# Moving sigmoid products and norm powers to GpSimd in a decoder layer of stick-breaking attention

## The chip, the core and the metric

The kernel runs on one core of a Trainium2 chip. The metric is the device time of one execution in microseconds (us); lower is better. The core has a matrix engine (PE in the rows; PEld is its weight load), a vector engine (DVE), a scalar engine (ACT), GpSimd (POOL), and a queue engine that issues the DMAs (SP). PE writes its results to PSUM, which DVE and ACT can read; everything else lies in SBUF.

## The reference

One decoder layer on an input of 2048 tokens by 1024 features, all in float32. Cut to what matters here:

```python
proj = x @ w_in                    # q, k, v (8 heads x 64), conv gates and h, pooling input
# stick-breaking attention, causal, per head, for query t and keys s < t
z = (q @ k.T) * 64 ** -0.5
log_om = where(s < t, log_sigmoid(-z), 0)
tail = reverse_cumsum(log_om) - log_om
a = where(s < t, exp(log_sigmoid(z) + tail), 0)
o = a @ v
# beside it: a short gated convolution and a multi-window pooling
mix = concat(o, conv, pooled)      # 1024 wide
mix = mix * rsqrt(mean64(mix * mix) + 1e-6) * gain      # norm of each group of 64
x = layer_norm(alpha * x + mix @ w_o)
x = layer_norm(alpha * x + relu(x @ w_up) ** 2 @ w_down)
```

A weight of the attention is thus a sigmoid of z times a product, over the keys between s and t, of sigmoids of -z.

## The kernel before

**Precision.** Each float32 operand of a large matmul is split in a rounded half (an ACT copy) and a remainder (a subtraction on DVE or GpSimd), and three matmuls stand for one. `load` (L163) does so for weights and inputs; its subtraction is L173, and `low_engine` deals it out between DVE and GpSimd by a count.

**Stages.** Tokens go in four chunks of 512. `qkv` projects q, k and v of two chunks at a time and `bchp` the convolution's and the pooling's inputs; both put their sums in the PSUM tag `dn` (`dense_ps`, two banks). `attention` works through 8 heads for each chunk. `out_stage` multiplies the normed mix with w_o for 16 row tiles of 128 tokens, also in `dn`, layer-norms each row tile, and `transposed` turns it around on PE for the feed-forward. Phase 2 is the feed-forward.

**One unit of the attention** (`unit`, L410 on) is a block of 128 queries by up to 512 keys: two matmuls make z in PSUM (tag `z`, two banks); ACT makes `beta`, the sigmoid of -z (L425, two tiles), and `sig`, the sigmoid of z (L427, two tiles); DVE runs a scan over beta from right to left (L432 for a diagonal block, L434 otherwise, which starts from the last product of the block to the right) into `g`; DVE multiplies g by sig in place (L436). There are 320 units, 128 of them diagonal. **One block** (`block`, L440 on), some units later, turns four g tiles around on PE (L453), splits the result (ACT L456 into `th`, DVE L457 into `tl`), and multiplies both halves with v (L458, L459).

**The norms.** `rsqrt` (L67) makes 1/sqrt(v + eps) for the 64-wide groups (32 times, tiles of 128x8, tags `rmsa`, `rmsb`) and for the first layer norm (16 times, 128x1, tag `ln`): a first value from the bits of the operand, then three Newton steps of three DVE instructions each (L73 to L75).

**The order.** The program is written with priorities: attention above the dense work (projections, output stage), and what empties a bank or feeds a load (`early`) above both. A scheduler then fixes one order of instructions for each engine, with its own estimates, so PE's row of instructions mixes attention and dense work; on the chip each engine runs its row strictly in order and waits where an operand isn't there.

Of the kernel before, what the change touches and what calls it, by code (L numbers as in the profile page):

```python
# [8 lines left out]

F = mybir.dt.float32  # L10
R = mybir.dt.float32r
I = mybir.dt.int32
AF = mybir.ActivationFunctionType
ALU = mybir.AluOpType
PSUM = bass.MemoryType.PSUM
# [2 lines left out]
P = 128  # L18
# [10 lines left out]
ALPHA = 2.0 ** 0.25  # L29
LN_EPS = 1e-5  # L30
RMS_EPS = 1e-6
SEED = 1.8352578724e-20
OFF = 8
START = 40
GROUPS = (9, 7, 8, 6)
# [6 lines left out]
def build(nc, tc, ctx, A, out):  # L42
# [16 lines left out]
    def split(dst_hi, dst_lo, src, scale=None):  # L59
# [3 lines left out]
        else:  # L63
            nc.scalar.activation(dst_hi, src, AF.Identity, scale=scale)
            nc.vector.scalar_tensor_tensor(dst_lo, src, scale, dst_hi.bitcast(F), ALU.mult, ALU.subtract)

    def rsqrt(pool, var, eps, shape, tag):  # L67
        """1 / sqrt(var + eps): a first value from the bits of the operand, then three Newton steps."""
        v, s, t = (pool.tile(shape, F, name=f"{tag}{k}", tag=f"{tag}{k}", bufs=2) for k in "vst")
        nc.vector.tensor_scalar(v, var, eps, None, ALU.add)  # L70
        nc.vector.tensor_scalar(s.bitcast(I), v.bitcast(I), 1, 0x7FFFFFFF, ALU.logical_shift_right, ALU.bitwise_xor)
        for _ in range(3):
            nc.vector.scalar_tensor_tensor(t, s, SEED * SEED, s, ALU.mult, ALU.mult)  # L73
            nc.vector.scalar_tensor_tensor(t, t, -0.5, v, ALU.mult, ALU.mult)
            nc.vector.scalar_tensor_tensor(s, t, 1.5, s, ALU.add, ALU.mult)  # L75
        return s

    def ln_stats(p, t, inverse):
# [5 lines left out]
        return mv[:, 0:1], inverse(p, mv[:, 1:2])  # L84

    def inverse_dve(p, var):
        s = rsqrt(p, var, LN_EPS, [P, 1], "ln")
        nc.vector.tensor_scalar(s, s, SEED, None, ALU.mult)
        return s

    def inverse_act(p, var):
        y, t = (p.tile([P, 1], F, name=f"ln{k}", tag=f"ln{k}", bufs=2) for k in "yt")
# [25 lines left out]
def phase1(nc, tc, ctx, A, ident, scr, split, rsqrt, layer_norm, bcast):  # L118
# [55 lines left out]
        return h, l  # L174

    def load_w(g, x=None):
        """The halves of group g of w_in, with the tiles of chunk x between them as the products take them."""
        w, xt = [], []
        with early():
            for q in range(4):  # L180
                w.append(load(A["w_in"][g][q], "w", [P, 2, 256], ND))
                if x is not None:
                    xt += [load_x(x, d) for d in (2 * q, 2 * q + 1)]
        return w, xt
# [17 lines left out]
        return ppd.tile([P, CH], F, name="dn", tag="dn", bufs=2)  # L202

    def operands(xs, g):
        """Yields the halves of group g of w_in with those of x for each chunk, loaded at the first use."""
        w = None
        for c, x in xs:
            if w is None:
                w, xt = load_w(g, None if x else c)
                x += xt  # L210
            elif not x:
                with early():
                    x += [load_x(c, d) for d in range(ND)]
            yield c, w, x
# [55 lines left out]
    def rms(m, j, c, ps_of, who):  # L270
# [4 lines left out]
        def rest(then, sink=lambda y: nc.sync.dma_start(mscr[c][j], y)):  # L275
            with early():
                var = ps_of()
                for t in range(4):
                    nc.tensor.matmul(var[:, 2 * t:2 * t + 2], sq[:, t * P:(t + 1) * P], blk, start=True, stop=True)
                y = rsqrt(pool, var[:, 0:8], RMS_EPS, [P, 8], f"rms{who[0]}")  # L280
                wide = sq.rearrange("p (g e) -> p g e", g=8)
                nc.scalar.activation(wide, y.unsqueeze(2).to_broadcast([P, 8, HD]), AF.Copy, scale=SEED)

            def scaled():
                with early():
                    ps = ps_of()
                    for t in range(4):
                        ts = slice(t * P, (t + 1) * P)
                        nc.tensor.transpose(out=ps[:, ts], in_=sq[:, ts], identity=ident)
                    o = pool.tile([P, CH], F, name=f"o{who}", tag=f"rms{who[0]}y", bufs=len(who))  # L290
                    nc.vector.scalar_tensor_tensor(o, m, gain[:, j:j + 1], ps, ALU.mult, ALU.mult)
                    sink(o)
            then(scaled)
# [83 lines left out]
                head(c, 2 * i + hh, mix)  # L377

    def run(end=False):
        """Emits the queued score tiles, each block of weights a few of them later."""  # L380
        while units:
            units.pop(0)()
            turn[0] += 1
# [24 lines left out]
    def unit(c, h, sg, m, j, st, start):  # L408
# [22 lines left out]
        if diag:  # L431
            nc.vector.tensor_tensor_scan(left, rev, last[:, :CH + OFF - w - 2:-1], 0.0, ALU.mult, ALU.add)  # L432
        else:
            nc.vector.tensor_tensor_scan(left, rev, rev, st["prev"][j][:, OFF - 1:OFF], ALU.mult, ALU.bypass)  # L434
        gv = g[:, OFF:OFF + w]
        nc.vector.tensor_tensor(gv, gv, sig[:, 0:w], ALU.mult)  # L436
        st["prev"][j] = g
        m["g"].append(g)

# [133 lines left out]

    def transposed(c, t, r):
        for dd in range(2):
            tp = spare_ps().rearrange("p (i t) -> p i t", i=4)
            for i in range(4):
                d = 4 * dd + i
                nc.tensor.transpose(out=tp[:, i, :], in_=r[:, d * P:(d + 1) * P], identity=ident)
            th = pd.tile([P, 4, P], R, name="x1h", tag="cs", bufs=4)  # L580
            tl = pd.tile([P, 4, P], R, name="x1l", tag="cs", bufs=4)
            with early():
# [39 lines left out]
class FeedForward:  # L622
# [20 lines left out]
        return [[t[:, d] for d in range(ND)] for t in w]  # L643

    def hidden(self, f, w=None):
        """Squared relu of the up projection for hidden tile f, in halves."""
        nc, p = self.nc, self.p
        wh, wl = w or self.up(f)
        hh = p.tile([P, HALF], R, name="hh", tag="hh", bufs=4)
# [15 lines left out]
        return hh, hl  # L665

    def rows(self, f):
        """The rows of w_down for hidden tile f, in halves."""
        return self.split(self.pd.tile([P, D], R, name="dh", tag="dh", bufs=4),
                          self.pd.tile([P, D], R, name="dl", tag="dl", bufs=4),  # L670
                          self.raw(self.A["w_down"][f * P:(f + 1) * P, :]))
# [97 lines left out]
```

## Time and profile before

| what | value |
|---|---|
| median of 3 runs | 2614.52 us (2614.03 to 2614.55) |
| span of the profiled execution | 2613.2 us |
| PE busy | 2519.7 us, 96% of the span |
| DVE busy | 1718.6 us, 66% |
| ACT busy | 982.4 us, 38% |
| POOL busy | 558.9 us, 21% |
| mean granted PE clock | 0.987 |

[...] Attention, mixed with projections, runs from about 10 to 1020 us; the rest of the output stage follows until about 1220 us, and the feed-forward from there to the end.

### The profile page before, as it was taken

To read this page: it belongs to the slowest core of one execution; us is meant where nothing else is said; L and a number is where in the kernel's file an instruction comes from. 1 tells how busy PE (TensorE), PEld (TensorE's weight loads), DVE (VectorE), ACT (ScalarE), POOL (GpSimd) and SP (SyncE) were. 2 spreads that over 40 slices of the span, in tenths; PEclk is the share of its full clock that TensorE was granted. 3 is DMA by queue.
4 is the path that set the end of the run, shared out by engine and by line. 5 is a ranking of instruction groups with operands and counts; after the bars stand their busy time and mean duration, and the time that the engine had idled before them with its cause. 6 is when DMAs were issued, how large, how long until landed. Compare 5 with 4: busy or idle time off the path is not lost. (4 is left out here: it accounts for less than half of the span.)

```text
span 2613.2 us, 32747 instructions
## 1 busy us (share of the span) xinstructions
PE 2519.7 (96%) x12112; PEld 2080.0 (80%) x12112; DVE 1718.6 (66%) x2839; ACT 982.4 (38%) x1802; POOL 558.9 (21%) x293
## 2 busy tenths in 40 slices
PE   8999999889989988999999999999999999999998
PEld 7887888768767767878888888888888888888886
DVE  4899999999999998875444444443564444444437
ACT  4667666656566563212221212121332121212122
POOL 2012000330131030211221212121342121212122
PEclk9999999999999999999999999999999999999999
DMA  8658545523342342668211111110541111111111
GB/s 243 176 153 227 151 134 142 180 74 101 101 121 78 93 133 90 229 215 322 91 57 41 57 41 57 41 57 25 217 154 57 41 57 41 57 41 57 41 41 65
DMA packets 131584, 280.63 MB, mean 107 GB/s; under 512 B 14944, under 2 KB 31328, under 8 KB 130400
## 3 DMA queue, kind: packets, MB, share of 16 engines
q1 hardware_dynamic: 131424, 278.54, 33.8%
q8 instruction: 95, 1.56, 0.2%
q14 instruction: 65, 0.53, 0.1%
HBM read 211.64 MB, written 66.85 MB: 107 GB/s over the span
## 5 line engine op out<-in xcount | busy, mean ns | idle before, releaser
L704 DVE TENSOR_TENSOR y<-dn,y 128x512 f32<-128x512 f32 x448 | 303.9, 686 | 367.0 <-PE dn L679 366.6
L677 PE MATMUL dn<-dh,hh 128*128 128x512 f32 x1024 | 398.3, 389 | 0.6 <-ACT hh L662 0.6
L678 PE MATMUL dn<-dl,hh 128*128 128x512 f32 x1024 | 398.4, 389 | 0.0
L679 PE MATMUL dn<-dh,hl 128*128 128x512 f32 x1024 | 398.2, 389 | 0.0
L656 PE MATMUL up<-x,uh 128*128 128x512 f32 x1008 | 392.3, 389 | 0.0
L657 PE MATMUL up<-x,uh 128*128 128x512 f32 x1008 | 392.2, 389 | 0.0
L663 DVE SCALAR_TENSOR_TENSOR rl<-up,rl 128x512 f32<-128x512 f32 x128 | 88.5, 691 | 374.6 <-ACT hh L662 374.6
L632 POOL TENSOR_TENSOR ul<-raw,uh 128x1024 fp32r<-128x1024 f32 x63 | 152.0, 2414 | 770.1 <-PE up L659 608.5
L661 ACT ACTIVATE rl<-up 128x512 f32<-128x512 f32 x128 | 76.2, 596 | 498.0 <-PE up L659 498.0
L434 DVE TENSOR_TENSOR_SCAN g<-beta,g 128x513 f32<-128x513 f32 x192 | 257.1, 1344 | 1.4 <-ACT beta L425 1.2
L659 PE MATMUL up<-x,ul 128*128 128x512 f32 x1008 | 256.2, 389 | 0.0
L173 POOL TENSOR_TENSOR wl<-wraw,wh 128x512 fp32r<-128x512 f32 x67 | 104.6, 1567 | 622.4 <-ACT wh L171 372.1
L436 DVE TENSOR_TENSOR g<-g,sig 128x512 f32<-128x512 f32 (+2 forms) x320 | 223.1, 702 | 11.4
L677 PEld LDWEIGHTS dn<-dh,hh 128*128 128x128 f32 x1024 | 192.2, 188 | 41.2 <-ACT hh L662 1.0
L679 PEld LDWEIGHTS dn<-dh,hl 128*128 128x128 f32 x1024 | 192.1, 188 | 40.3 <-DVE hl L664 0.4
L678 PEld LDWEIGHTS dn<-dl,hh 128*128 128x128 f32 x1024 | 192.2, 188 | 39.9
L224 PE MATMUL dn<-xh,wh 128*128 128x512 f32 x512 | 211.9, 416 | 11.4 <-ACT xh L171 4.8
L659 PEld LDWEIGHTS up<-x,ul 128*128 128x128 f32 x1008 | 189.2, 188 | 39.3
L657 PEld LDWEIGHTS up<-x,uh 128*128 128x128 f32 x1008 | 189.2, 188 | 39.3
L656 PEld LDWEIGHTS up<-x,uh 128*128 128x128 f32 x1008 | 189.2, 188 | 39.2
L225 PE MATMUL dn<-xl,wh 128*128 128x512 f32 x512 | 209.9, 410 | 0.1
L425 ACT ACTIVATE beta<-z 128x512 f32<-128x512 f32 (+2 forms) x320 | 173.4, 542 | 96.7 <-PE z L422 56.0
(159 smaller groups left out, 4603.8 us busy)
## 6 DMA issues: line engine op xcount, KB each, us to landing
raw<-in_w_down SPq DMA_DIRECT2D x64, 512.0 KB, 3.3
raw<-in_w_up SPq DMA_DIRECT2D x63, 512.0 KB, 3.3
wraw<-in_w_in SPq DMA_DIRECT2D x80, 256.0 KB, 3.0
k<-kscr SPq DMA_DIRECT2D x80, 256.0 KB, 3.1
v<-vscr SPq DMA_DIRECT2D x80, 256.0 KB, 2.8
xraw<-in_xt SPq DMA_DIRECT2D x64, 256.0 KB, 3.0
q<-qscr SPq DMA_DIRECT2D x64, 256.0 KB, 4.3
x<-tscr SPq DMA_DIRECT2D x8, 2048.0 KB, 12.3
```

The source lines that it names most:

```text
L224: nc.tensor.matmul(ps, wh, xh, start=(d == 0), stop=False)
L225: nc.tensor.matmul(ps, wh, xl, start=False, stop=False)
L425: nc.scalar.activation(beta[:, CH - w:CH], z[:, 0:w], AF.Sigmoid, scale=-1.0)
L434: nc.vector.tensor_tensor_scan(left, rev, rev, st["prev"][j][:, OFF - 1:OFF], ALU.mult, ALU.bypass)
L436: nc.vector.tensor_tensor(gv, gv, sig[:, 0:w], ALU.mult)
L656: nc.tensor.matmul(ps, wh[d], xh[:, :, d, :], start=(d == 0), stop=False)
L657: nc.tensor.matmul(ps, wh[d], xl[:, :, d, :], start=False, stop=False)
L659: nc.tensor.matmul(ps, wl[d], xh[:, :, d, :], start=False, stop=(d == ND - 1))
L677: self.nc.tensor.matmul(ps, hh[:, ts], dh[:, ds], start=(i == 0), stop=False)
L678: self.nc.tensor.matmul(ps, hh[:, ts], dl[:, ds], start=False, stop=False)
L679: self.nc.tensor.matmul(ps, hl[:, ts], dh[:, ds], start=False, stop=(i == len(hid) - 1))
L704: nc.vector.tensor_tensor(y[t][:, ds], ps, y[t][:, ds], ALU.add)
```

## The change

Four edits in one. (1) The product of g and sig goes from DVE to GpSimd. (2) The scan of a non-diagonal block got beta twice as its inputs, the second of them unused (`bypass`); it now gets one column of z, broadcast, so that its second input lies in PSUM. (3) `rsqrt` takes its first value from a power on GpSimd, and one Newton step instead of three follows; the constant SEED that scaled the old first value is gone, and with it the last DVE instruction of the layer norm's `inverse_dve`. (4) `transposed` puts its results in the two `dn` banks instead of the attention's `tp` banks (three) or, at the end, two banks of its own, and its transposes get the high priority of `early`.

```diff
@@ build
+    expo = const.tile([P, 8], F, name="expo")
+    nc.vector.memset(expo, -0.5)
+
     def rsqrt(pool, var, eps, shape, tag):
         v, s, t = (pool.tile(shape, F, name=f"{tag}{k}", tag=f"{tag}{k}", bufs=2) for k in "vst")
         nc.vector.tensor_scalar(v, var, eps, None, ALU.add)
-        nc.vector.tensor_scalar(s.bitcast(I), v.bitcast(I), 1, 0x7FFFFFFF, ALU.logical_shift_right, ALU.bitwise_xor)
-        for _ in range(3):
-            nc.vector.scalar_tensor_tensor(t, s, SEED * SEED, s, ALU.mult, ALU.mult)
-            nc.vector.scalar_tensor_tensor(t, t, -0.5, v, ALU.mult, ALU.mult)
-            nc.vector.scalar_tensor_tensor(s, t, 1.5, s, ALU.add, ALU.mult)
+        nc.gpsimd.tensor_tensor(s, v, expo[:, 0:shape[1]], ALU.pow)
+        nc.vector.scalar_tensor_tensor(t, s, -0.5, v, ALU.mult, ALU.mult)
+        nc.vector.scalar_tensor_tensor(t, t, 0.0, s, ALU.add, ALU.mult)
+        nc.vector.scalar_tensor_tensor(s, t, 1.5, s, ALU.add, ALU.mult)
         return s
...
     def inverse_dve(p, var):
-        s = rsqrt(p, var, LN_EPS, [P, 1], "ln")
-        nc.vector.tensor_scalar(s, s, SEED, None, ALU.mult)
-        return s
+        return rsqrt(p, var, LN_EPS, [P, 1], "ln")
...
@@ unit
         else:
-            nc.vector.tensor_tensor_scan(left, rev, rev, st["prev"][j][:, OFF - 1:OFF], ALU.mult, ALU.bypass)
+            idle = z[:, 0:1].to_broadcast([P, CH + 1])
+            nc.vector.tensor_tensor_scan(left, rev, idle, st["prev"][j][:, OFF - 1:OFF], ALU.mult, ALU.bypass)
         gv = g[:, OFF:OFF + w]
-        nc.vector.tensor_tensor(gv, gv, sig[:, 0:w], ALU.mult)
+        nc.gpsimd.tensor_tensor(gv, gv, sig[:, 0:w], ALU.mult)
...
@@ transposed
         for dd in range(2):
-            tp = spare_ps().rearrange("p (i t) -> p i t", i=4)
-            for i in range(4):
-                d = 4 * dd + i
-                nc.tensor.transpose(out=tp[:, i, :], in_=r[:, d * P:(d + 1) * P], identity=ident)
+            with early():
+                tp = dense_ps().rearrange("p (i t) -> p i t", i=4)
+                for i in range(4):
+                    d = 4 * dd + i
+                    nc.tensor.transpose(out=tp[:, i, :], in_=r[:, d * P:(d + 1) * P], identity=ident)
```

In the middle of the attention DVE's row of instructions before is this (scan L434, product L436, `tl` L457, pooling L349, a Newton step L75):

```order
L457 TENSOR_TENSOR tl<-tp,th 128x256
L434 SCALAR_TENSOR_TENSOR g<-beta_242,g 128x513
L436 TENSOR_TENSOR g<-g,sig 128x512
L349 SCALAR_TENSOR_TENSOR pl<-pb,pa 64x512
L75 SCALAR_TENSOR_TENSOR rmsbs<-rmsbt,rmsbs 128x8
L434 SCALAR_TENSOR_TENSOR g<-beta_240,g 128x513
L349 SCALAR_TENSOR_TENSOR pl<-pc,pa 64x512
L436 TENSOR_TENSOR g<-g,sig 128x512 x2
```

After the change DVE's row at a like place is this (scan L433, now with z among its inputs; `tl` L456; a gate L352):

```order
L433 SCALAR_TENSOR_TENSOR g<-beta_242,g,z 128x513
L456 TENSOR_TENSOR tl<-tp,th 128x128
L433 SCALAR_TENSOR_TENSOR g<-beta_244,g,z 128x513
L456 TENSOR_TENSOR tl<-tp,th 128x512 x2
L352 TENSOR_TENSOR cs<-dn,cs 128x512
L433 SCALAR_TENSOR_TENSOR g<-beta_242,g,z 128x513
L456 TENSOR_TENSOR tl<-tp,th 128x512
L433 SCALAR_TENSOR_TENSOR g<-beta_244,g,z 128x513
```

The products have left DVE's row. They stand in GpSimd's, which had only the subtractions of L173 and the pooling's sums; late in the attention it now reads (product L435, subtraction L171, power L72):

```order
L171 TENSOR_TENSOR wl<-wraw,wh 128x512
L435 TENSOR_TENSOR g<-g,sig 128x512
L171 TENSOR_TENSOR wl<-wraw,wh 128x512
L435 TENSOR_TENSOR g<-g,sig 128x512
L171 TENSOR_TENSOR wl<-wraw,wh 128x512
L435 TENSOR_TENSOR g<-g,sig 128x512
L171 TENSOR_TENSOR wl<-wraw,wh 128x512 x2
L72 TENSOR_TENSOR lns<-lnv,expo 128x1
```

Products wait behind subtractions there, one for one in the densest places.

On PE, at a row tile of the output stage after the attention, the eight transposes (L579) of before stand together and write a tile of their own (`xt`), between the products L509 to L511 into `dn`:

```order
L510 MATMUL dn<-xl,wh 128x512
L511 MATMUL dn<-xh,wl 128x512
L579 MATMUL xt<-ident,r 128x128 x8
L509 MATMUL dn<-xh,wh 128x512
L510 MATMUL dn<-xl,wh 128x512
```

After the change they write `dn`, in two groups of four around the last matmul of a product (L508 to L510 now):

```order
L508 MATMUL dn<-xh,wh 128x512
L509 MATMUL dn<-xl,wh 128x512
L579 MATMUL dn<-ident,r 128x128 x4
L510 MATMUL dn<-xh,wl 128x512
L579 MATMUL dn<-ident,r 128x128 x4
L508 MATMUL dn<-xh,wh 128x512
```

The second group follows the first at the distance of one matmul, with only two banks for both and the products. In all, 60 of the 128 transposes and 429 of the 768 output products now stand ahead of the attention's last matmul in PE's row; before it were none and 68.

## Rows read from the trace of the kernel before

**Rows 1.** The page, part 1: busy us, share of the span, instructions of each engine

```profile
PE 2519.7 (96%) x12112; PEld 2080.0 (80%) x12112; DVE 1718.6 (66%) x2839; ACT 982.4 (38%) x1802; POOL 558.9 (21%) x293
```

**Rows 2.** Stretches: start:end, length, busy of each engine (instructions), PE clock, DMA share, GB/s

```profile
0.00:100.00 100.00, 91.80 (x506) 78.32 (x507) 59.70 (x98) 51.60 (x105) 17.36 (x22) 1.00 0.79 230
100.00:500.00 400.00, 384.49 (x2276) 331.55 (x2275) 383.40 (x622) 264.54 (x559) 59.38 (x37) 0.98 0.57 158
500.00:1000.00 500.00, 452.11 (x2277) 358.18 (x2276) 490.54 (x840) 307.95 (x616) 116.53 (x74) 0.96 0.35 106
1000.00:1050.00 50.00, 44.32 (x200) 35.19 (x199) 37.67 (x94) 12.78 (x23) 0.64 (x1) 0.93 0.36 118
1050.00:1100.00 50.00, 50.00 (x233) 40.66 (x232) 40.58 (x98) 10.23 (x19) 9.13 (x8) 1.00 0.62 212
1100.00:1250.00 150.00, 147.07 (x678) 119.26 (x677) 102.21 (x246) 32.71 (x52) 32.57 (x18) 1.00 0.75 265
1250.00:2613.00 1363.00, 1349.91 (x5953) 1116.80 (x5952) 604.54 (x846) 302.60 (x430) 323.30 (x135) 1.00 0.18 63
```

**Rows 3.** Waits, 500 to 1000 us: engine, line, awaited line, us, times, longest

```profile
PE o L459 <- DVE tl L457: 13.9, 18, 2.0
PE tp L453 <- DVE tl L457: 8.8, 6, 3.1
PE o L458 <- DVE mixr L473: 6.1, 3, 4.2
```

**Rows 4.** Groups by line: shapes, count, busy us, mean ns, idle before and its releasers

```profile
L436 DVE TENSOR_TENSOR g<-g,sig 128x512 f32<-128x512 f32 (+2 forms) x320 | 223.1, 702 | 11.4
L434 DVE TENSOR_TENSOR_SCAN g<-beta,g 128x513 f32<-128x513 f32 x192 | 257.1, 1344 | 1.4 <-ACT beta L425 1.2
L457 DVE TENSOR_TENSOR tl<-tp,th 128x512 fp32r<-128x512 f32 x224 | 149.4, 678 | 2.9 <-ACT th L456 2.8
L427 ACT ACTIVATE sig<-z 128x512 f32<-128x512 f32 (+2 forms) x320 | 172.8, 540 | 60.7 <-DVE g L436 42.4 <-DVE rmsbt L73 4.2 <-DVE rmsat L73 2.7
```

**Rows 5.** Groups by line: the norm's small DVE steps, largest and smallest, and first value

```profile
L75 DVE SCALAR_TENSOR_TENSOR rmsbs<-rmsbt,rmsbs 128x8 f32<-128x8 f32 x48 | 12.3, 257 | 0.2
L73 DVE SCALAR_TENSOR_TENSOR rmsat<-rmsas 128x8 f32<-128x8 f32 x48 | 9.2, 191 | 0.6
L71 DVE TENSOR_SCALAR rmsbs<-rmsbv 128x8 int32<-128x8 int32 x16 | 4.7, 296 | 0.1
```

**Rows 6.** Timeline of DVE and POOL, 506 to 516 us: start, us, what

```profile
506.23 0.68 DVE L436 TENSOR_TENSOR g<-g,sig 128x512 f32<-128x512 f32 x1
507.43 1.27 DVE L434 TENSOR_TENSOR_SCAN g<-beta,g 128x513 f32<-128x513 f32 x1
...
510.26 1.78 DVE L436 TENSOR_TENSOR g<-g,sig 128x512 f32<-128x512 f32 x1
511.96 0.68 DVE L62 TENSOR_TENSOR vst<-dn,vst 128x512 fp32r<-128x512 f32 x1
...
507.47 4.02 POOL L173 TENSOR_TENSOR xl<-xraw,xh 128x512 fp32r<-128x512 f32 x2 [4.09 <-ACT xh L171]
```

**Rows 7.** Groups by line: products and subtractions that GpSimd already does

```profile
L562 POOL TENSOR_TENSOR upl<-upraw,uph 128x512 fp32r<-128x512 f32 x2 | 2.6, 1291 | 1.3 <-ACT uph L561 1.3
L173 POOL TENSOR_TENSOR wl<-wraw,wh 128x512 fp32r<-128x512 f32 x67 | 104.6, 1567 | 622.4 <-ACT wh L171 372.1 <-PE dn L510 107.0 <-DMA kscr<-qk 34.6
L632 POOL TENSOR_TENSOR dl<-raw,dh 128x1024 fp32r<-128x1024 f32 x64 | 153.5, 2400 | 256.2 <-ACT dh L631 256.2
```

**Rows 8.** Timeline at one row tile's transposes and their split, 1091 to 1095 us

```profile
1091.62 0.40 PE L510 MATMUL dn<-xl,wh 128*128 128x512 f32 x1
...
1091.85 1.03 PE L579 MATMUL xt<-ident,r 128*128 128x128 f32 x8
...
1092.49 1.08 ACT L61 CAST x1h<-xt 128x512 fp32r<-128x512 f32 x2 [11.52 <-PE xt L579]
...
1093.33 0.68 DVE L62 TENSOR_TENSOR x1l<-xt,x1h 128x512 fp32r<-128x512 f32 x1
```

More of the change, by code (lines that the diff above doesn't have):

```diff
@@ L11 @@
 R = mybir.dt.float32r
-I = mybir.dt.int32
 AF = mybir.ActivationFunctionType
@@ L31 @@
 RMS_EPS = 1e-6
-SEED = 1.8352578724e-20
 OFF = 8
@@ L281, in rest @@
                 wide = sq.rearrange("p (g e) -> p g e", g=8)
-                nc.scalar.activation(wide, y.unsqueeze(2).to_broadcast([P, 8, HD]), AF.Copy, scale=SEED)
+                nc.scalar.activation(wide, y.unsqueeze(2).to_broadcast([P, 8, HD]), AF.Copy)
             def scaled():
```

## Prediction

> **What bounds the kernel now.** I read the busy line first [rows 1]: PE is 96% busy, which seems to leave 4%. The table of stretches [rows 2] says where that lies. From 1250 us on PE is busy 1349.9 of 1363 us at full clock; the feed-forward gives nothing, and no edit touches it. From 100 to 1050 us, where attention runs, PE is idle 15.5 + 47.9 + 5.7 = 69.1 us, and its granted clock falls below 1.00: means of 0.98, 0.96 and 0.93, so 0.02 x 400 + 0.04 x 500 + 0.07 x 50 = 31.5 us more are lost at the lower of the two levels (1.2 instead of 2.4 GHz). Together 100.6 us; this is what a change here can win. Idle time at the low clock is counted twice in it, and short gaps hidden in the matmuls' records not at all, so I take it as it is.
>
> In the same stretches DVE is busy 383.4 of 400 and 490.5 of 500 us [rows 2], and PE's longest sums of waits are for DVE: `tl`, then `tl` again, then the attention's output [rows 3]. So DVE bounds the attention, and PE, whose row is filled with dense work between, waits for it. Where DVE is less full, PE loses little: from 1050 to 1250 us DVE is busy 142.8 of 200 us (71%) and PE idle 2.9 us (1.5%), at full clock. With DVE at 96% (100 to 500 us) PE loses 15.5 + 8 = 23.5 of 400 us (5.9%).
>
> **The change part by part.** *Products.* They take 223.1 us of DVE [rows 4], all inside the attention. On GpSimd a 128x512 instruction of two inputs takes 1.291 us undisturbed and a 128x1024 one 2.400 us [rows 7], so some 0.18 us and 2.17 ns a column: 224 products of 512 columns cost 289 us, and 32 each of 128, 256 and 384 columns 71 us; 360 us in all. GpSimd is now busy 17.4 + 59.4 + 116.5 + 0.6 = 193.9 us until 1050 us [rows 2]; with the products 554 us of about 985, so it has room. Its instructions are on no path by themselves: a g tile is transposed some units after its product.
>
> *Scan.* A DVE instruction with both inputs in SBUF is held while GpSimd works: a product took 1.78 us inside a GpSimd subtraction and 0.68 us outside, while one with an input in PSUM took 0.68 us beside that subtraction [rows 6]. So edit 2 keeps 192 scans from being held by the products that edit 1 puts beside them. It frees the difference between the mean of 1.344 us [rows 4] and the 1.27 us of a free one [rows 6], 192 x 0.07 = 13 us. Whether the PSUM input slows the scan no row shows; nearest is `tl`, which reads PSUM and takes a mean of 0.678 us for 512 columns [rows 4] against the product's free 0.68 us [rows 6], so I take nothing; the ends are nothing and 0.1 us a scan, 19 us of DVE. [...] The z bank is now held until the scan, so a z matmul two units on can wait for DVE; the units lie about 985 / 320 = 3.1 us apart and two sigmoids (0.54 us) and a scan fit in twice that, so I take nothing, at most 10 us.
>
> *Norms.* The six groups of Newton steps on 128x8 run from 12.3 down to 9.2 us and sum to 63.3 us [rows 5]; two thirds go, 42 us, and the first values with 8.5 us (4.7 of them in rows 5): 51 us of DVE in the attention. Layer norms save some 23 us, mostly where PE is full anyway. The power on 128x8 stands in no row. By its columns alone it would cost 0.2 us on GpSimd; as it must be many steps I take 1 us, and 2.4 us, the longest group [rows 7], as the upper end: 32 to 77 us of GpSimd, still covered. A power also waits in GpSimd's row behind products, but nothing urgent hangs on a norm; its transposes come blocks later.
>
> *Order and banks.* The transposes no longer queue behind the attention's `tp` banks, so 361 output products (0.23 to 0.24 us from start to start) and 60 transposes (eight in 0.8 to 1.0 us) [rows 8] move ahead of the attention's end: some 91 us of PE work to fill gaps with, and about 56 us of DVE work of the output stage with it. The price is the two `dn` banks. At five of the last row tiles the second group of transposes, or the product behind it, needs a bank that the first has just filled. It is free when ACT and DVE have split it: the rows show the transposes' start at 1091.85, ACT's first copy from 1092.49 and the first remainder done at 1094.01 [rows 8], so some 1.7 us after a group of four ends; a matmul or two lie between. I take 1.4 us x 5 = 7 us, between 0 and 12.
>
> *The sum.* DVE's work until the attention's end is now 59.7 + 383.4 + 490.5 + 37.7 = 971.3 us [rows 2]. Less 223, 13 and 51, plus 56: 740 us. Some 400 two-input instructions stay on DVE (diagonal scans, subtractions, norm steps, the convolution), and GpSimd is busy 554 + 32 = 586 of 985 us, 60%, not 18%. Held half a GpSimd instruction (0.65 us) in the extra 42% of cases, they cost 105 us more: 845 us of 985, 86%. Between the two stretches above (71%: 1.5% lost; 96%: 5.9%) that gives 4.1% of PE's time lost. PE's work there is 950 - 100.6 + 91, some 940 us plus its losses: 40 us lost. So 100.6 + 1.4 (the loss that the moved work had at its old place) - 40 - 7 = 55 us are won: 2613.2 - 55 = 2558 us. The median of the runs is 1.3 us above the span; I predict **2559 us**.
>
> **Rivals.** *PE full.* If DVE's waits are fewer than I reckon, PE loses 1.5% throughout, 14 us: 2613.2 - (100.6 + 1.4 - 14 - 7) = 2532, with the median 2533 us. For it speaks that PE is then the fullest engine by far; against it that diagonal scans and subtractions are still held. *Waits stay.* PE's row is in a fixed order; if held instructions make DVE and GpSimd late by turns, the loss may be 8%, 75 us, and 2613.2 - 20 = 2593, 2594 us. For it speaks that 500 to 1000 us lost 13.6%, and that GpSimd was busiest there.
>
> *GpSimd as the gate, slower than before.* `sig` has two tiles, so ACT's sigmoid two units on waits for the product, and ACT's queue holds the `th` copies and bank evacuations behind it, for which PE waits. ACT already waited 42.4 us for DVE's products there [rows 4]. Now the product takes 1.29 us, more when held, and stands behind subtractions of 1.57 us [rows 7]; a unit's turn of 3.1 us holds one of each. If e us of each unit reach PE, the time is 2559 + 320 e: it decides from e = 0.17 us, and at 0.3 us gives 2655 us. Against it: g is needed only units later, and GpSimd has 40% to spare. [...] *A slow power.* The change would not do what it says if the power takes many us: each of 32 would hold the products behind it. With about 2 us of slack at each, x us cost 32 (x - 2); from 3.7 us this eats the gain, and at 6 us it gives 2687 us. No row speaks for it, none excludes it.
>
> **How the numbers follow.** Forecast (2540 to 2580 us) 45%; PE full (under 2540) 20%; waits stay (2580 to 2610) 15%; GpSimd as the gate 13%; slow power 4%; the last 3% a tie by accident. Of the gate's and the power's 17% I give 2% to ends that cancel with the gain. So faster by over 0.2% 80%, within 0.2% 5%, slower 15%; 0.2% (5 us) is about what a measurement of this kernel can tell from no change. The range leaves out the 15% above and some 5% below: 2520 to 2612 us.
>
> **What would show it.** From 100 to 1000 us DVE falls from 96% to under 90%, POOL rises to about 60%, PE's idle time falls to a third and its clock stays at 1.00 but for a few moments; non-diagonal scans stand at 1.27 us with no spread; products at 1.3 to 1.8 us on POOL; the power at about 1 us; at the last row tiles PE waits 1 to 2 us for the split. It would be wrong if ACT's sigmoid waits for POOL for over 100 us, if the power takes over 4 us, or if the scan got slower by over 0.1 us.

## The result, and the profile after

The changed kernel takes 2547.89 us (median of 4 runs, 2545.92 to 2552.0) against 2614.53 us for the kernel before on the same chip: a ratio of 0.9744, with a 95% interval from 0.973 to 0.9758. That is 66.6 us less; the forecast was 2559 us, 55 us less, in a range from 2520 to 2612 us. The profiled execution spans 2546.3 us at a mean granted clock of 0.995, against 2613.2 us at 0.987.

The page's first part, for the changed kernel (busy us, share of the span, instructions), answers to [rows 1]:

```profile
PE 2491.7 (98%) x12112; PEld 2067.3 (81%) x12112; DVE 1520.9 (60%) x2168; ACT 977.7 (38%) x1802; POOL 975.3 (38%) x661
```

DVE lost 197.7 us and POOL gained 416.4 us. PE's idle time, span less busy, fell from 93.5 to 54.6 us, 38.9 us; its busy time fell by 28.0 us with the same 12112 matmuls. Together they are the 66.9 us between the spans. Where they lie is read from the stretches of the changed kernel (columns as in [rows 2], which they answer):

```profile
0.00:100.00 100.00, 92.21 (x509) 79.43 (x510) 55.34 (x82) 53.28 (x108) 38.55 (x43) 1.00 0.80 232
100.00:500.00 400.00, 393.15 (x2347) 342.16 (x2346) 311.05 (x421) 265.54 (x563) 242.35 (x200) 0.99 0.60 168
500.00:1000.00 500.00, 479.58 (x2484) 387.11 (x2483) 434.16 (x616) 304.31 (x615) 315.67 (x246) 0.99 0.40 125
1000.00:1050.00 50.00, 48.27 (x250) 39.78 (x249) 42.88 (x72) 22.95 (x44) 20.38 (x16) 1.00 0.55 179
1200.00:2546.00 1346.00, 1332.67 (x5877) 1102.51 (x5875) 598.53 (x838) 300.26 (x427) 320.95 (x134) 1.00 0.18 62
```

From 100 to 1050 us PE is idle 6.85 + 20.42 + 1.73 = 29.0 us, and the lower clock costs 0.01 x 400 + 0.01 x 500 = 9 us: 38 us lost, where it was 100.6 us. By this reckoning, which counts idle time at the low clock twice, 62.6 of the 66.9 us were won in the attention. Behind 1200 us PE is idle 1% of the time, as it was. The lower clock also accounts for most of the fall of PE's busy time: 9 us of that loss instead of 31.5 is 22.5 of the 28.0 us.

What PE still waits for in the attention, from the waits of PE between 100 and 1100 us (line, awaited line, us, times, longest), which answers to [rows 3]:

```profile
PE z L420 <- DVE g L433: 12.0, 13, 2.4
PE o L458 <- DVE tl L456: 2.5, 5, 1.1
PE dn L579 <- DVE r L541: 2.4, 3, 1.2
```

The `tl` waits of [rows 3] are all but gone. The longest sum is new: a matmul into a z bank that waits for the scan (L433), because that scan now reads z. The next fence is from the groups by line of the changed kernel and answers to [rows 4]: the non-diagonal scan, the product, and `tl`.

```profile
L433 DVE TENSOR_TENSOR_SCAN g<-beta,g,z 128x513 f32<-128x513 f32 x192 | 243.9, 1275 | 51.1 <-ACT sig L425 49.2 <-PE tp L452 1.6
L435 POOL TENSOR_TENSOR g<-g,sig 128x512 f32<-128x512 f32 x224 | 296.3, 1325 | 273.5 <-DVE g L433 165.9 <-DVE g L430 19.7 <-PE tp L452 15.7
L456 DVE TENSOR_TENSOR tl<-tp,th 128x512 fp32r<-128x512 f32 x224 | 146.9, 676 | 19.7 <-ACT th L455 19.2
```

The scan's mean fell from 1344 to 1275 ns, but DVE now idles 49.2 us ahead of scans for `sig`; ahead of the old scan it idled 1.4 us in all. The old scan needed only `beta`. The new one reads the z bank, which ACT reads last for `sig`, and in this program it starts behind that; with the old inputs put back (below) the waits for `sig` are gone and the scan waits for `beta` again.

The power, in groups of the changed kernel (L72; the layer norm's on 128x1 included), which answers to the question that [rows 7] could only bound:

```profile
L72 POOL TENSOR_TENSOR rmsbs<-rmsbv,expo 128x8 f32<-128x8 f32 x16 | 28.0, 1750 | 6.4 <-DVE rmsbv L71 6.4
L72 POOL TENSOR_TENSOR rmsas<-rmsav,expo 128x8 f32<-128x8 f32 x16 | 27.0, 1690 | 6.1 <-DVE rmsav L71 6.1
L72 POOL TENSOR_TENSOR lns<-lnv,expo 128x1 f32<-128x1 f32 x16 | 14.8, 928 | 87.2 <-DVE lnv L71 87.2
```

Last, ACT's waits between 100 and 1050 us in the changed kernel. They show that the feared gate did not close: the sigmoid waits for GpSimd's products 8.9 us in all, 1.0 us at the longest.

```profile
ACT beta L423 <- PE z L420: 155.3, 113, 5.0
ACT sig L425 <- POOL g L435: 8.9, 15, 1.0
```

ACT now waits for PE, 155.3 us; DVE waits for ACT. PE is the fullest engine of the attention.

How one engine holds the other is seen in a timeline of the changed kernel, DVE and then POOL between 701 and 708 us (start, us, what):

```profile
703.34 1.27 DVE L433 TENSOR_TENSOR_SCAN g<-beta,g,z 128x513 f32<-128x513 f32 x1
704.52 0.13 DVE L73 SCALAR_TENSOR_TENSOR rmsbt<-rmsbs,rmsbv 128x8 f32<-128x8 f32 x1
704.58 0.68 DVE L456 TENSOR_TENSOR tl<-tp,th 128x512 fp32r<-128x512 f32 x1
705.18 0.80 DVE L74 SCALAR_TENSOR_TENSOR rmsbt<-rmsbt,rmsbs 128x8 f32<-128x8 f32 x1
706.02 1.20 DVE L75 SCALAR_TENSOR_TENSOR rmsbs<-rmsbt,rmsbs 128x8 f32<-128x8 f32 x1
...
703.32 2.64 POOL L435 TENSOR_TENSOR g<-g,sig 128x512 f32<-128x512 f32 x2
705.92 2.50 POOL L171 TENSOR_TENSOR wl<-wraw,wh 128x512 fp32r<-128x512 f32 x2
```

The scan and `tl` have their free durations while POOL works on products. The two small Newton steps, L74 and L75, are of eight columns and have both inputs in SBUF; one that isn't held takes 0.13 us, as L73 does just ahead, on the border between the two products. L74 ends at 705.98 us, when the second product ends (705.96), and L75 at 707.22 us, about when the first subtraction does (half of 2.50 us after 705.92 is 707.17). Each was held for most of a GpSimd instruction, 0.7 and 1.1 us. In [rows 6] the subtraction into `vst` starts at 511.96 us, when GpSimd's last subtraction there has ended (507.47 + 4.02 = 511.49 us), so that row didn't show an instruction with an input in PSUM beside GpSimd's work, as I read it; here `tl` shows it, 0.68 us from 704.58 us on while GpSimd multiplies from 703.32 to 705.96 us.

### The profile page after: what moved, and what is told of

Read it like the earlier page. It is cut to its first block, busy times and chain, and to the rows that moved or that the text cites. A ratio compares the mean times of both kernels' runs of the same rounds, so it can differ in the third digit from the quotient of the medians.

```text
span 2546.3 us, 32552 instructions
## 1 busy us (share of the span) xinstructions
PE 2491.7 (98%) x12112; PEld 2067.3 (81%) x12112; DVE 1520.9 (60%) x2168; ACT 977.7 (38%) x1802; POOL 975.3 (38%) x661
## 5 line engine op out<-in xcount | busy, mean ns | idle before, releaser
L435 POOL TENSOR_TENSOR g<-g,sig 128x512 f32<-128x512 f32 (+2 forms) x320 | 377.8, 1185 | 353.8 <-DVE g L433 165.9
L433 DVE TENSOR_TENSOR_SCAN g<-beta,g,z 128x513 f32<-128x513 f32 x192 | 243.9, 1275 | 51.1 <-ACT sig L425 49.2
L632 POOL TENSOR_TENSOR dl<-raw,dh 128x1024 fp32r<-128x1024 f32 x64 | 153.5, 2400 | 255.0 <-ACT dh L631 255.0
L420 PE MATMUL z<-k,q 128*128 128x512 f32 (+3 forms) x640 | 193.5, 382 | 16.0 <-DVE g L433 12.0
```

The lines of the kernel that those rows point to most:

```text
L420: nc.tensor.matmul(z[:, 0:w], q[:, b, j * P:(j + 1) * P], m["k"][:, 0:w], start=(b == 0), stop=(b == 1))
L433: nc.vector.tensor_tensor_scan(left, rev, idle, st["prev"][j][:, OFF - 1:OFF], ALU.mult, ALU.bypass)
L435: nc.gpsimd.tensor_tensor(gv, gv, sig[:, 0:w], ALU.mult)
L632: self.nc.gpsimd.tensor_tensor(lo, raw, hi.bitcast(F), ALU.subtract)
```

## The experiments

A difference between a kernel and the changed one is that of their ratios to the kernel before, times 2614.5 us. Each edit undone also gives the scheduler other costs, so the order of the engines' rows moves too; two samples below say how much that alone is worth.

### Each edit undone by itself

**Products back on DVE** (line numbers in rows are each kernel's own):

```diff
-        nc.gpsimd.tensor_tensor(gv, gv, sig[:, 0:w], ALU.mult)
+        nc.vector.tensor_tensor(gv, gv, sig[:, 0:w], ALU.mult)
```

> The changed kernel with edit 1 undone: the 320 products of g and sig are back on DVE, the other three edits stay. Theory (the gain is DVE's relief, and the products carry most of it): DVE's work in the attention rises by some 220 us to over 95% of the stretch 100 to 1000 us, and the time goes to 2590 to 2615 us. Rival (the gain is the output stage's work that edit 4 let into the attention as a filler): the time stays at 2545 to 2565 us.

Measured: 0.9844 (0.983 to 0.9859), 2577.0 us; 26 us more than the change. Both expectations missed: DVE comes to 93% of 100 to 1000 us, not over 95%, and the time lies between the two ranges. DVE is busier in the late attention than in any other kernel here but the one before, and PE loses little more. The stretch from 500 to 1000 us of this kernel:

```profile
500.00:1000.00 500.00, 480.00 (x2457) 386.06 (x2456) 472.40 (x753) 296.13 (x595) 140.53 (x94) 0.98 0.40 123
```

With 472.4 of 500 us DVE is 94% busy, and PE is idle 20.0 us, as in the change (20.4). The 26 us lie mostly elsewhere, half of them behind the attention: its last matmul starts at 1083.5 us instead of 1041.8, 525 output products stand ahead of it instead of 429, and from 1100 to 1250 us PE is idle 9.6 us at a clock of 0.97, where the change has 1.4 us at 1.00. So edits 2, 3 and 4 without the products give 41 us of the gain; taking 223 us off DVE adds 26.

**The scan with two SBUF inputs again:**

```diff
-            idle = z[:, 0:1].to_broadcast([P, CH + 1])
-            nc.vector.tensor_tensor_scan(left, rev, idle, st["prev"][j][:, OFF - 1:OFF], ALU.mult, ALU.bypass)
+            nc.vector.tensor_tensor_scan(left, rev, rev, st["prev"][j][:, OFF - 1:OFF], ALU.mult, ALU.bypass)
```

> The changed kernel with edit 2 undone: the non-diagonal scan has beta as both inputs again. Theory (GpSimd's products now hold any DVE instruction with two SBUF inputs): the 192 scans rise from a mean of 1.28 us by 0.3 to 0.45 us, DVE gains 60 to 85 us, the time goes to 2565 to 2590 us. Rival (the z bank that is held until the scan costs as much as the held scans): PE's waits of z for the scan, 12 us now, go to nothing and the time stays at 2538 to 2552 us.

Measured: 1.0044 (1.0029 to 1.0059), 2629.8 us: slower than the kernel before, and 78 us slower than the change, nearly twice the 42 us that were expected at the most. In its groups the scan and the product both grew:

```profile
L432 DVE TENSOR_TENSOR_SCAN g<-beta,g 128x513 f32<-128x513 f32 x192 | 309.4, 1620 | 24.3 <-ACT beta L423 23.1 <-PE tp L451 0.5
L434 POOL TENSOR_TENSOR g<-g,sig 128x512 f32<-128x512 f32 (+2 forms) x320 | 420.2, 1321 | 283.8 <-DVE g L432 72.7 <-DVE g L430 61.8 <-ACT sig L425 23.1
```

The scan went from 1275 to 1620 ns, 65 us in all; the product, over all its shapes, from 1185 to 1321 ns (377.8 to 420.2 us), 42 us. So GpSimd is held by DVE's two-input instructions as well, and not only the other way. The rival's condition is met and its time isn't: the 12.0 us that PE waited on z for the scan are gone, but 12.6 us of waits on z for `sig` stand in their place. Its waits of PE between 100 and 1100 us and of ACT between 100 and 1050 us show the rest:

```profile
PE o L457 <- DVE tl L455: 17.4, 19, 4.5
PE tp L451 <- POOL g L434: 17.2, 17, 1.8
...
ACT sig L425 <- POOL g L434: 54.7, 52, 2.9
```

PE waits for products, and ACT's sigmoid waits for them six times as long as in the change: the chain of the rival "GpSimd as the gate" appears as soon as scan and product hold each other. Part of the 78 us is order: the scheduler moved 96 output products ahead of the attention's end in this kernel, not 429. How the 78 us part between the two no run shows.

**The old first value and three Newton steps on DVE:**

```diff
-        nc.gpsimd.tensor_tensor(s, v, expo[:, 0:shape[1]], ALU.pow)
-        nc.vector.scalar_tensor_tensor(t, s, -0.5, v, ALU.mult, ALU.mult)
-        nc.vector.scalar_tensor_tensor(t, t, 0.0, s, ALU.add, ALU.mult)
-        nc.vector.scalar_tensor_tensor(s, t, 1.5, s, ALU.add, ALU.mult)
+        nc.vector.tensor_scalar(s.bitcast(I), v.bitcast(I), 1, 0x7FFFFFFF, ALU.logical_shift_right, ALU.bitwise_xor)
+        for _ in range(3):
+            nc.vector.scalar_tensor_tensor(t, s, SEED * SEED, s, ALU.mult, ALU.mult)
+            nc.vector.scalar_tensor_tensor(t, t, -0.5, v, ALU.mult, ALU.mult)
+            nc.vector.scalar_tensor_tensor(s, t, 1.5, s, ALU.add, ALU.mult)
...
```

> The changed kernel with edit 3 undone: bits and three Newton steps on DVE, no power on GpSimd. Theory: 51 us of small steps, more when held, come back to a DVE that is about 85% full, and 55 us of powers leave GpSimd; the time rises by 3 to 15 us to 2551 to 2563 us. Rival (the powers, 1.7 us each in GpSimd's row, cost as much as the steps that they save): 2540 to 2549 us.

Measured: 0.9949 (0.9933 to 0.9966), 2604.2 us, 54 us more than the change; both expectations missed. Its late stretch, its longest wait of PE (100 to 1100 us), one of its groups and a wait of ACT (100 to 1100 us):

```profile
500.00:1000.00 500.00, 462.93 (x2331) 372.05 (x2329) 451.02 (x743) 294.89 (x595) 271.94 (x216) 0.96 0.37 111
...
PE z L422 <- DVE g L435: 17.7, 17, 3.3
...
L73 DVE SCALAR_TENSOR_TENSOR rmsbt<-rmsbs 128x8 f32<-128x8 f32 x48 | 21.0, 437 | 0.9
...
ACT sqb L282 <- DVE rmsbs L75: 40.8, 15, 7.7
```

The step L73 took a mean of 212 ns in the kernel before and takes 437 ns here, beside a GpSimd that has the products. DVE is busy 451.0 us of this stretch, only 16.9 us more than in the change, yet PE is idle 37.1 us and its clock 0.96: 37.1 + 20 = 57 us lost, where the change loses 20.4 + 5 = 25. Nine dependent steps in a row, whose groups' means are 241 to 437 ns here and were 191 to 257 ns in the kernel before, make what stands behind them on DVE late, and the ACT instruction that reads the result waits for them 40.8 us in all, up to 7.7 us at a time.

**The transposes in their own banks, without priority** (edit 4 undone):

```diff
-            with early():
-                tp = dense_ps().rearrange("p (i t) -> p i t", i=4)
+            tp = spare_ps().rearrange("p (i t) -> p i t", i=4)
```

> The changed kernel with edit 4 undone: the normed rows are transposed in the attention's banks again, at low priority. Theory (the order lets 91 us less of dense work into the attention, so PE has less to fill waits with): the time rises by 15 to 40 us to 2563 to 2588 us, though the waits at the last row tiles (5 us) go. Rival (the filler isn't needed once DVE has room): 2538 to 2550 us.

Measured: 0.9825 (0.981 to 0.9839), 2571.5 us, 21 us more than the change, as the theory has it. Here 192 output products stand ahead of the attention's end instead of 429. The stretch from 500 to 1000 us:

```profile
500.00:1000.00 500.00, 468.93 (x2388) 372.72 (x2386) 426.04 (x584) 310.27 (x629) 322.29 (x251) 0.97 0.36 108
```

PE is idle 31.1 us at a clock of 0.97, where the change has 20.4 us at 0.99, though DVE is a little less busy than in the change. That PE lacks work there to fill gaps with fits both, but the run doesn't part it from the change of banks.

### Which part of the norm's edit counts

**The power, and three Newton steps behind it:**

```diff
-        nc.vector.scalar_tensor_tensor(t, s, -0.5, v, ALU.mult, ALU.mult)
-        nc.vector.scalar_tensor_tensor(t, t, 0.0, s, ALU.add, ALU.mult)
-        nc.vector.scalar_tensor_tensor(s, t, 1.5, s, ALU.add, ALU.mult)
+        for _ in range(3):
+            nc.vector.scalar_tensor_tensor(t, s, -0.5, v, ALU.mult, ALU.mult)
+            nc.vector.scalar_tensor_tensor(t, t, 0.0, s, ALU.add, ALU.mult)
+            nc.vector.scalar_tensor_tensor(s, t, 1.5, s, ALU.add, ALU.mult)
```

> The changed kernel with three Newton steps behind the power instead of one: 288 more small DVE instructions with two SBUF inputs, GpSimd's row as after. Theory (the 53 us that undoing edit 3 cost are small steps held by GpSimd, each in a chain that stops DVE's row): the steps' mean stays well over 0.16 us and the time goes to 2585 to 2610 us. Rival (the cost came from the first value's place or from a row of PE that fell out worse by chance): 2545 to 2565 us.

Measured: 0.9922 (0.9905 to 0.9938), 2596.2 us, 47 us more than the change, as the theory has it; the steps' means are 264 to 510 ns. That is nearly all of the 54 us that edit 3 is worth, with GpSimd's work as in the change (975.9 against 975.3 us). So most of the price lies in the small steps that stand in a chain on DVE, not in where the first value is made. The order is not the same (384 output products ahead of the attention's end, not 429), but one of the two samples below has the same 384 and costs 12 us, not 47. ACT's waits between 100 and 1050 us in this kernel:

```profile
ACT sqa L281 <- DVE rmsas L76: 42.1, 14, 7.2
ACT sqb L281 <- DVE rmsbs L76: 40.5, 15, 5.9
```

In the change these two are 15.8 and 25.6 us; in the kernel before, with nine steps but a GpSimd that is busy 19% of the time beside them, they were 20.3 and 22.3 us.

**The power alone.** This kernel leaves out the Newton step, a part of the norm's computation:

```diff
-        nc.vector.scalar_tensor_tensor(t, s, -0.5, v, ALU.mult, ALU.mult)
-        nc.vector.scalar_tensor_tensor(t, t, 0.0, s, ALU.add, ALU.mult)
-        nc.vector.scalar_tensor_tensor(s, t, 1.5, s, ALU.add, ALU.mult)
```

> The changed kernel without the Newton step, so the power's own value is used: 144 fewer small DVE instructions. Theory (held small steps): the time falls by 5 to 20 us to 2528 to 2545 us. Rival (chance of the order): 2543 to 2560 us, either side of the changed kernel.

Measured: 0.9756 (0.9742 to 0.9771), 2553.3 us; the interval overlaps that of the change, so taking out the last three steps gains nothing, as the rival has it. Its late stretch is the best of all here:

```profile
500.00:1000.00 500.00, 483.74 (x2544) 393.05 (x2543) 422.85 (x555) 315.93 (x637) 334.11 (x256) 1.00 0.40 126
```

PE loses 16.3 us there at full clock, 9 less than in the change. Over the whole span, though, PE idles 2552.1 - 2491.9 = 60.2 us, more than the 54.6 of the change: the gain is given back elsewhere, most of it from 1100 to 1250 us, where PE is idle 8.2 us at a clock of 0.97 (1.4 us at 1.00 in the change). Whether that is the order alone no run shows.

**Each power twice:**

```diff
+        nc.gpsimd.tensor_tensor(t, v, expo[:, 0:shape[1]], ALU.pow)
         nc.gpsimd.tensor_tensor(s, v, expo[:, 0:shape[1]], ALU.pow)
```

> The changed kernel with each power made twice, the first into a tile that is overwritten: 48 more GpSimd instructions, some 70 us, in front of the norm's steps. Theory (GpSimd has 40% to spare and a norm is urgent for nobody): the time stays at 2545 to 2560 us. Rival (GpSimd is near being the gate): over 2565 us.

Measured: 0.9868 (0.9853 to 0.9882), 2581.9 us, 32 us more; the theory is wrong, and the rival's side is met. Some 66 us of GpSimd (1041.6 against 975.3 us) cost half of that in time, though GpSimd has room in the mean. A group of this kernel, and ACT's wait for a norm (100 to 1050 us):

```profile
L74 DVE SCALAR_TENSOR_TENSOR rmsbt<-rmsbs,rmsbv 128x8 f32<-128x8 f32 x16 | 14.7, 921 | 1.1 <-POOL rmsbs L73 1.1
...
ACT sqb L281 <- DVE rmsbs L76: 38.5, 14, 5.4
```

The step after the power, 592 ns in the change, takes 921 ns. So a longer power is not covered, as the prediction had it: the norm's chain is longer by it, and GpSimd's other work is late by it.

### The banks

**Own banks for the last chunk's transposes:**

```diff
-                tp = dense_ps().rearrange("p (i t) -> p i t", i=4)
+                tp = (spare_ps() if c == NC - 1 else dense_ps()).rearrange("p (i t) -> p i t", i=4)
```

> The changed kernel, but the row tiles of the last chunk are transposed in the two banks that are free by then. Theory (the 5 us of PE's waits at the last row tiles are for a dn bank): these waits go and the time falls by 3 to 6 us to 2541 to 2546 us. Rival (something else is late there, or the waits only move): no change, 2546 to 2551 us.

Measured: 0.9735 (0.9721 to 0.975), 2547.9 us, the same as the change. The transposes behind 1000 us in this kernel, by the bank that they write, and PE's waits there:

```profile
L579 PE MATMUL dn<-ident,r x56: 270/272/328, 1004.1 to 1101.2; 128*128 128x128 f32 x56
L579 PE MATMUL xt<-ident,r x32: 270/272/273, 1110.2 to 1148.2; 128*128 128x128 f32 x32
...
PE dn L579 <- DVE r L541: 2.9, 4, 1.2
PE dn L508 <- DVE r L541: 1.7, 2, 1.0
```

The 32 transposes that got banks of their own were not those that waited. The waits are those of transposes before 1101.2 us that still use `dn`, and they wait for `r` (L541), the addition that empties the bank of a product, not for the split of the transposes ahead. They are 3.1 + 1.7 us in the change and 2.9 + 1.7 us here.

**A third z bank** in place of a third `tp` bank, against the new wait of z for the scan:

```diff
-        z = pp.tile([P, CH], F, name="z", tag="z", bufs=2)
+        z = pp.tile([P, CH], F, name="z", tag="z", bufs=3)
...
-        tp = pp.tile([P, CH], F, name="tp", tag="tp", bufs=3)
+        tp = pp.tile([P, CH], F, name="tp", tag="tp", bufs=2)
```

> The changed kernel with three z banks and two tp banks instead of two and three. Theory (what is left of PE's waits is the z bank that edit 2 holds until the scan, 12 us on PE and more behind it): PE's waits of z for the scan go under 4 us and the time falls to 2525 to 2543 us. Rival (the tp banks are needed as much, so the wait changes its place): 2545 to 2580 us, with PE or ACT waiting for tl.

Measured: 0.9895 (0.988 to 0.991), 2588.2 us, 40 us more. The theory is wrong; the rival has the direction, but the time lies beyond its range and the waits that grew most are not for `tl`. PE's longest wait and three of ACT's between 100 and 1100 us:

```profile
PE z L420 <- DVE g L433: 17.6, 26, 4.2
...
ACT th L455 <- PE tp L452: 99.5, 71, 6.6
ACT sig L425 <- POOL g L435: 71.0, 102, 2.5
ACT beta L423 <- DVE g L433: 37.9, 52, 4.0
```

In the change these were 12.0, 44.9, 8.9 and 1.5 us. PE's waits of z for the scan did not go but rose, and ACT now waits for the tiles of `sig` and `beta`, of which there are two each, as well as for `tp`. So this run doesn't price the z bank: what its wait costs by itself stays open.

### Products alone, and the order

**The kernel before with edit 1 only:**

```diff
-        nc.vector.tensor_tensor(gv, gv, sig[:, 0:w], ALU.mult)
+        nc.gpsimd.tensor_tensor(gv, gv, sig[:, 0:w], ALU.mult)
```

> The kernel before with edit 1 alone: the products on GpSimd, scans with two SBUF inputs, three Newton steps on DVE, transposes in the attention's banks. Theory (GpSimd's products hold every DVE instruction with two SBUF inputs, and are held by them): the 192 scans rise to 1.6 us or more, the Newton steps to over 0.4 us, and the time is at or above the kernel before, 2615 to 2680 us. Rival (moving 223 us of DVE's work away pays by itself): 2560 to 2605 us.

Measured: 1.0025 (1.0016 to 1.0034), 2622.7 us: 6.5 us slower, more than the noise of repeated runs but less than the order alone is worth (below). So edit 1 by itself gains nothing that shows, as the theory has it, though the scans stay just under its 1.6 us and the Newton steps, at means of 296 to 489 ns, are mostly under its 0.4 us. Two groups and ACT's wait for products (100 to 1050 us):

```profile
L434 DVE TENSOR_TENSOR_SCAN g<-beta,g 128x513 f32<-128x513 f32 x192 | 301.2, 1575 | 15.4 <-ACT beta L425 11.3 <-PE tp L453 2.8 <-POOL xl L173 0.7
L436 POOL TENSOR_TENSOR g<-g,sig 128x512 f32<-128x512 f32 (+2 forms) x320 | 420.4, 1322 | 365.8 <-DVE g L434 78.9 <-DVE g L432 47.4 <-ACT beta L425 38.4
...
ACT sig L427 <- POOL g L436: 68.9, 60, 3.5
```

Of the 223 us taken from DVE 44 come back as longer scans, and ACT and PE wait for products. The edit that looks largest by its load is worth nothing here on its own; in the change it stands together with scans that are out of GpSimd's way (a mean of 1275 ns), with shorter norms, and with edit 4.

**Two samples of the order.** `START` says from which load on the dealing of subtractions between DVE and GpSimd turns over; three more or fewer move one of them and let the scheduler find another order.

```diff
-START = 40
+START = 43
```

> The changed kernel with one of 191 subtractions moved from GpSimd to DVE near the start, which changes no load to speak of (1 us) but lets the scheduler come to another order. It measures what an order that fell out otherwise is worth. Theory (the 20 to 79 us of the undone edits and of the doubled power are their own): within 8 us of the changed kernel, 2540 to 2556 us. Rival (much of those differences is chance of the order): over 10 us away.

> The changed kernel with one of 191 subtractions moved the other way, from DVE to GpSimd near the start: a second sample of the order. Theory: 2540 to 2556 us. Rival (chance of the order): over 10 us away from the changed kernel.

Measured: 0.9766 (0.9751 to 0.9781), 2555.0 us, with 43, and 0.979 (0.9774 to 0.9807), 2559.6 us, with 37: 6 and 12 us more than the change. The first is within what was expected, the second is not and meets the rival. One subtraction is about 1.4 us of work, so this is what the order alone is worth. The change as measured has the best of three orders; differences of 12 us or less between the kernels above say nothing about an edit, and of the larger ones an unknown part is order, since each kernel was run with one order only.

## Why the prediction was right

**What bounds.** The loss was where [rows 2] and [rows 3] put it. In the attention 38 us are lost against 40 forecast, and the feed-forward did not move. PE's idle time there fell from 69.1 to 29.0 us, to 42% rather than a third, and the clock is at 0.99 to 1.00. The loss at the lower clock is reckoned from its granted share alone, and no run shows a clock in GHz; the trace of the kernel before shows the share at 1.00 from 476 to 478 us and at 0.50 from 482 to 484 us.

**Terms of the sum, by their order:**

| step | forecast | measured |
|---|---|---|
| products on GpSimd | 360 us, 1.29 us a 512 | 377.8 us, 1.325 us |
| GpSimd until 1050 us | 586 us | 617 us, 59% |
| scan | 1.27 us, no spread | 1.275 us, 1.287 at most |
| scan from PSUM | nothing, up to 0.1 us | nothing |
| power on 128x8 | 1 us (0.2 to 2.4) | 1.72 us |
| z bank held | nothing (up to 10 us) | 12.0 us of PE's waits |
| DVE until the attention's end | 845 us | 843.4 us until 1050 us |
| `dn` banks | 7 us (0 to 12) | 4.8 us |
| loss of PE | 40 us | 38 us |

Whether a scan is slower with an input in PSUM, which the rows of before left open, the change decides: 1275 ns from PSUM against 1.27 us for a free one from SBUF in [rows 6].

**What was mis-sized.** The 1 us of the power was my estimate, with no row behind it, and why a power takes the time that it takes no run shows; it takes 1.7 times what I took, 1.69 to 1.75 us, inside the bounds, and it was not free: doubled, it costs 32 us, not nothing. My slack formula, 32 (x - 2), named the wrong object; what a longer power delays is GpSimd's row and the norm's chain. The z bank was put at nothing, with 10 us as the end, and PE waits 12.0 us for it; and I did not see that the scan, once it reads z, stands behind `sig` too: 49.2 us of DVE's idle time, which DVE could afford at 78 to 87% busy. The bank price was about right in size and wrong in cause: PE waits for the addition of a product, not for the split. The norms' steps on 128x8, put at 51 us less DVE, saved 25 (71.8 us before, 46.8 after), because the steps that are left are held: the six groups' means are 236 to 674 ns. The 845 us of DVE agree with the measured 843.4 in part by luck: they were set against 985 us, 86%, while the attention's last matmul starts at 1041.8 us and DVE is busy 83% of 100 to 1050 us.

**What was right by a wrong split.** The sum treats the edits as loads on one engine that add up. They don't. Undone one at a time, they cost 26, 78, 54 and 21 us, 179 in all, where the whole gains 67. By its load edit 1 was the largest (223 us of DVE), and by itself it gains nothing; edit 2 was put at 13 us of DVE and is worth 78, some of it order; edit 4 stands in the sum only as more work for DVE and as waits for banks, and undoing it costs 21 us. What stood behind the sum, a PE loss read from DVE's busy share, holds for the change (87% of 500 to 1000 us: the line between the two stretches gives 4.3%, measured 5.1%), and fails across kernels. From 500 to 1000 us, idle time of PE and the loss at the lower clock together (the clock is given to 0.01, so half a point is rounding), and the output products that stand ahead of the attention's last matmul in PE's row:

| kernel | DVE busy | PE's loss | output products ahead |
|---|---|---|---|
| before | 98% | 13.6% | 68 |
| products back on DVE | 94% | 6.0% | 525 |
| products alone | 94% | 16.5% | 103 |
| old norms | 90% | 11.4% | 357 |
| two SBUF inputs | 90% | 14.8% | 96 |
| power and three steps | 89% | 9.0% | 384 |
| power twice | 87% | 8.9% | 360 |
| the change | 87% | 5.1% | 429 |
| order, 43 | 87% | 4.8% | 429 |
| order, 37 | 86% | 6.2% | 384 |
| transposes apart | 85% | 9.2% | 192 |
| power, no step | 85% | 3.3% | 379 |
| third z bank | 83% | 5.3% | 618 |

At 94% the loss is 6.0% or 16.5%. Two things part these kernels, and the runs do not separate them. One is whether the scans, on which each unit's product, `sig` tile and z bank hang, are held: the mean scan is 1277 ns in the first and 1575 ns in the second. The other is how much dense work PE's row holds to fill its waits: the four kernels with fewer than 200 output products ahead have four of the five largest losses, and one of them, the transposes apart, has free scans and short chains. For the norms the runs say more: among the five kernels with 357 to 384 products ahead the loss is 3.3% without the step, 6.2% in a sample of the order, 8.9% with the power twice, 9.0% with three steps and 11.4% with the old norms. I read this as the price of held instructions in chains; for the scans it is argued, not shown apart from the order. The sum came to 55 of 67 us although several of its terms are wrong: with the measured 38 us and 4.8 us for its two losses it gives 59, and three orders of the changed kernel gain between 55 and 67 us, so a forecast that near is partly luck.

**The rivals.** "PE full" (2533 us) and "waits stay" (2594 us) both lie further off than the forecast. "GpSimd as the gate" did not decide in the change, at 8.9 us of waits, but it was no idle fear: with the scan held it shows at once, 54.7 and 68.9 us. "A slow power" was excluded by its 1.7 us. The forecast lies among the three orders that were run: 2548, 2555 and 2560 us.

**Open.** How much of the 78 us of the scan is the holding's and how much the missing dense work's; how much of the 32 us of the doubled power and of the gain that leaving out the step did not bring is the order's; and the price of the z bank's wait.

## What to carry to other kernels

Before work goes from DVE to GpSimd, look at what stays on DVE with both inputs in SBUF, above all at instructions in a dependent chain: give them an operand in PSUM, or shorten the chain, in the same change, since the move alone gained nothing here (a ratio of 1.0025, with the scans' mean at 1575 instead of 1344 ns). Price an edit by what waits behind the instruction, not by its own microseconds, and see what work the other engine's row holds to fill those waits. And where a scheduler sets the order, run two or three orders before a difference of half a per cent is put down to an edit.

## What the runs showed of the hardware

- A broadcast column of PSUM as a scan's unused second input costs the scan nothing that shows (1275 ns for 513 columns, against 1.27 us for a free one from SBUF) and takes it out of GpSimd's way (1287 ns at most, with GpSimd busy 59% of the time until 1050 us); the same scan with two SBUF inputs beside GpSimd's products has a mean of 1575 to 1620 ns.
- The holding goes both ways: beside such scans GpSimd's products, over all their shapes, grow from a mean of 1185 to 1321 ns.
- Two DVE steps of eight columns with both inputs in SBUF took 0.80 and 1.20 us where one that wasn't held took 0.13 us, and ended within 0.05 us of the GpSimd instruction beside them.
- A power on GpSimd took a mean of 1.69 to 1.75 us for 128x8 and 0.93 us for 128x1 in the change, where a product took 0.56 us for 128x128.
